# A hybrid decoder step: four sequences' states updated in one piece, and two read-outs turned together

## The chip, the cores and the metric

The kernel runs on one core of one Trainium2 chip. The core has five engines that run their own instruction queues beside each other: TensorE (PE, matmuls and transposes; PEld is its weight load), VectorE (DVE), ScalarE (ACT), GpSimd (POOL) and SyncE (SP), which here only issues transfers. Matmuls write into eight PSUM banks; everything else lives in SBUF or in HBM. The metric is the device time of one execution in microseconds (us), as the median of several runs.

## The reference

One layer of a decoder for a prompt of 1024 tokens and for 8 sample sequences of 8 tokens each, which bring their states along. A combined projection feeds a pooling branch and a Mamba-2 branch (SSD); both are gated and projected back. Cut to the part of the SSD that matters here:

```python
proj = h @ w_in                                   # 1024 -> 8224 columns
u_pool, z_pool, z_ssm, xbc, dt_raw, g_raw = split(proj)
xbc = silu(causal_conv(xbc)); xs, B, C = split(xbc)  # 32 heads of 64, 4 groups of B, C (128 states)
...
def step(h, inp):                                 # one chunk; for a sample: all its 8 tokens
    xq, dq, Bq, Cq = inp
    acs = cumsum(dq * Ag, axis=1)
    ...
    y = einsum('bijge,bjgep->bigep', att, xq)     # inside the chunk
    y = y + einsum('bign,bige,bgepn->bigep', Cq, exp(acs), h)          # read-out of the old state
    last = acs[:, -1]
    w_in = exp(last[:, None] - acs) * dq
    h = h * exp(last)[..., None, None] + einsum('bjgn,bjge,bjgep->bgepn', Bq, w_in, xq)   # update
    return h, y
```

For the 8 sample sequences the initial state `h` (8 × 32 heads × 64 × 128, 8 MB) is an input and the new one an output.

## The kernel before

The kernel goes through stages. First the input is normalised and split into high and low parts. Then the projection runs as Strassen products: `pair_w` loads two column blocks of the weights (`rawA`, three buffers, on SyncE's queue, L336), makes differences of them (L347, VectorE and GpSimd) and splits each into a rounded part `whi` (ScalarE, L145) and a rest `wlo` (GpSimd, L148); `product` (L410) makes two half products of twelve matmuls each, of 128×128 by 272 columns, into a PSUM bank, and VectorE adds the banks into the results (L419, L424). Banks come from three pools: `PA` (tag mm, three banks), `PB` (tag ps, four) and `PC` (tag pc, one). In this stage the half products take `PB` and `PA` in turn. Behind the projection come the prompt's SSD chunks, the branches' output projections (L221), the gates and the last projection (L2040 to L2042).

Beside the last ten pairs of columns of the projection, the generator `all_samples` is run: after each of some of the projection's steps it issues one more slot, up to its next `yield`, 28 slots in all. It computes the SSD of the 8 samples, group by group (four groups of B and C, each with 8 heads, so 512 columns of state for each sample), in two halves of four samples (`hf`):

- `load_h0(i)` loads the states of two samples (`h0`, 128 states × 2 × 512, two transfers on SyncE's queue, L1274); `begin` loads the group's rows; `rows` (L1285) turns x; `weigh` (L1294 to L1297) makes the weights inside the 8 tokens, `within` the part of the output from the tokens themselves.
- `spread(hf)` puts each sample's 8 columns of x and B into a stretch of 32 (GpSimd, L1307), and C's 8 columns into a zeroed `cz` of 4 × 32 (VectorE, L1309 and L1310). `split(hf)` turns x and B (L1318, L1320), scales them and rounds them with the rest beside them (L1322 to L1329) into a buffer of tag `dec`.
- `state(hf)` (L1344) multiplies the old states by `cz`: four samples, each 32 rows of one bank `PC`, of which 8 are of use. `out` (ScalarE, L1365) copies the bank, `end(hf)` turns it (four transposes, L1370), scales it (L1372) and adds it to the result (L1376), which goes out after the second half.
- `update(hf, e)` takes one half `e` of the heads, 256 columns: four 32-row matmuls (L1353) into four banks, GpSimd's multiplication of the old states by their decay (L1358), VectorE's adds from the banks (L1360), and the stores on ScalarE's queue (L1361).

TensorE's instructions stay in the order in which they are issued in this stage; on the other engines a scheduler places them within their dependencies. The slots before: `state(0)`, `out`, `update(0, 0)`; then `update(0, 1)`; then `end(0)`; then `state(1)`, `out`, `update(1, 0)`; then the next group's `rows` with `update(1, 1)` between; then `end(1)` at the head of the next group. `sp` is the pool in SBUF of the samples' buffers: three for `h0` (`H0B`), two for `dec`. Right behind the stage `ckt` takes the buffers of the chunks.

Of the kernel before, what the change touches and what calls it, by code (L numbers as in the profile page):

```python
# [9 lines left out]
F32R = mybir.dt.float32r  # L10
AF = mybir.ActivationFunctionType
ALU = mybir.AluOpType
# [8 lines left out]
P = 128  # L21
# [25 lines left out]
def tile_pool_ssd_step(  # L47
# [1049 lines left out]
        store_(new_conv[mc], t27)  # L1097
        yield 1

    H0B = 3  # L1100


    def dt_end():
# [161 lines left out]
    class Samples:  # L1265
# [23 lines left out]

        def weigh(self):  # L1290
            g, S, xb = self.g, NS, self.xb
            self.dec = dec = spt([P, 640], "dec", 2)[:S, :512].rearrange("p (h t) -> p h t", t=S)
            pc = PB()
            mm(pc[:S, :S], xb[:, 4], xb[:, 5], start=True, stop=True)  # L1294
            cb = pc[:S, S:2 * S]
            V.tensor_tensor(cb, pc[:S, :S], maskS.rearrange("p b i -> p (b i)"), ALU.mult)
            V.tensor_tensor(dec.rearrange("p h (b i) -> p h b i", i=8),  # L1297
                            Es[1][:, 8 * g:8 * g + 8].unsqueeze(2).to_broadcast([S, 8, NB, 8]),
                            cb.rearrange("p (b i) -> p b i", i=8).unsqueeze(1).to_broadcast([S, 8, NB, 8]), ALU.mult)

        def spread(self, hf):

            xb = self.xb
            rep = spt([P, 5, 4, 4, 8], "xw", 1)
            for b in range(4):
                o = 32 * hf + 8 * b
                nc.gpsimd.tensor_copy(rep[:, :, b], xb[:, 0:5, o:o + 8].unsqueeze(2).to_broadcast([P, 5, 4, 8]))  # L1307
            cz = spt([P, 4, 32], "cz", 2)
            V.memset(cz, 0.0)  # L1309
            V.tensor_copy(cz[:, :, 0:8], xb[:, 5, 32 * hf:32 * hf + 32].rearrange("p (b i) -> p b i", i=8))  # L1310
            self.half[hf] = rep, cz

        def split(self, hf):
            g = self.g
            rep, cz = self.half[hf]
            px = PB()
            for q in range(4):
                nc.tensor.transpose(px[:, q * P:(q + 1) * P], rep[:, q].rearrange("p b r i -> p (b r i)"), ident)  # L1318
# [3 lines left out]
            V.tensor_tensor(xs, px.rearrange("p (h d) -> p h d", d=64),  # L1322
                            wd3[:, hf, 8 * g:8 * g + 8].unsqueeze(2).to_broadcast([P, 8, 64]), ALU.mult)
            both = spt([P, 640], "dec", 2, F32R)
# [14 lines left out]
            V.tensor_tensor(t, inner(self.xd, self.dec, NS), t, ALU.add)  # L1339

        def state(self, hf):
            self.po = PC()
            for b in range(4):
                mm(self.po[32 * b:32 * b + 32, :], self.half[hf][2][:, b, :], self.h0[2 * hf + b // 2][:, b % 2], start=True, stop=True)  # L1344

        def update(self, hf, e):
            g = self.g
            xh, Bx, _ = self.half[hf]
            c = slice(256 * e, 256 * e + 256)
            pus = [p()[:, :256] for p in (PB, PA, PB, PA)]  # L1350
            for b in range(4):
                r = slice(32 * b, 32 * b + 32)
                mm(pus[b], Bx[r], xh[r, c], start=True, stop=True)  # L1353
            for i in range(2):
                j = 4 * hf + 2 * i
                h0 = self.h0[2 * hf + i]
                hv = h0[:, :, c].rearrange("p a (h d) -> p a h d", d=64)
                nc.gpsimd.tensor_tensor(hv, hv, ElS[:, j:j + 2, 8 * g + 4 * e:8 * g + 4 * e + 4].unsqueeze(3).to_broadcast([P, 2, 4, 64]), ALU.mult)  # L1358
                for a in range(2):
                    V.tensor_tensor(h0[:, a, c], h0[:, a, c], pus[2 * i + a], ALU.add)  # L1360
                store_(new_ssm_s[g, j:j + 2, :, c].rearrange("a p x -> p a x"), h0[:, :, c])  # L1361

        def out(self):
            self.yo = spt([P, 512], "hT", 1)
            act(self.yo, self.po, AF.Copy)  # L1365

        def end(self, hf):
            pn = PB()
            for q in range(4):
                nc.tensor.transpose(pn[:, q * P:(q + 1) * P], self.yo[:, q * P:(q + 1) * P], ident)  # L1370
            tn = spt([P, 4, 32], "tn", 1)
            V.tensor_tensor(tn.rearrange("p q (b i) -> p q b i", i=8),  # L1372
                            pn.rearrange("p (q b i) -> p q b i", q=4, i=32)[:, :, :, 0:8],
                            self.E2[:, :, 32 * hf:32 * hf + 32].rearrange("p q (b i) -> p q b i", i=8), ALU.mult)
            th = self.t[:, :, 32 * hf:32 * hf + 32]
            V.tensor_tensor(th, th, tn, ALU.add)  # L1376
            if hf:
                store_(ys_d[self.g], self.t)

    def all_samples():  # L1380
        gs_ = [Samples(g) for g in range(NG)]
        samples_load()
        gs_[0].begin()
        for i in range(2):
            gs_[0].load_h0(i)
        yield
        samples_decay()
        gs_[0].rows()
        gs_[0].spread(0)
        yield  # L1390
        gs_[0].split(0)
        gs_[0].weigh()
        yield
        for g, m in enumerate(gs_):
            n = gs_[g + 1] if g + 1 < NG else None
            if g:
                gs_[g - 1].end(1)
                m.split(0)
            m.within()
            if g:  # L1400
                m.load_h0(1)
# [24 lines left out]
            m.update(1, 1)  # L1426
            if n:
                n.weigh()
            yield
        gs_[-1].end(1)  # L1430
        yield

    def cc(m):
# [855 lines left out]
```

## Time and profile before

| | us |
|---|---|
| median of 3 runs | 1220.73 (1219.95 to 1222.36) |
| span of the profiled execution | 1219.3 |
| TensorE's busy time in it | 1203.2 |
| VectorE, GpSimd, ScalarE | 937.9, 758.1, 654.7 |

The profile is of one execution. Its rows have a start in us and a duration, then engine and line (L410 is line 410 of the kernel), the operation, result<-operands by the program's names, the shape, and a count of equal rows that were drawn together; brackets name idle time of the engine ahead of the row and what ended it. A row of a group has the count, the busy time, the mean of one in ns, and the idle time ahead. SPq is SyncE's queue of instructions, where transfers are issued. PEclk is the granted clock of TensorE, 1.00 for full.

### The profile page before, as it was taken

To read this page: it belongs to the slowest core of one execution; us is meant where nothing else is said; L and a number is where in the kernel's file an instruction comes from. 1 tells how busy PE (TensorE), PEld (TensorE's weight loads), DVE (VectorE), ACT (ScalarE), POOL (GpSimd) and SP (SyncE) were. 2 spreads that over 40 slices of the span, in tenths; PEclk is the share of its full clock that TensorE was granted. 3 is DMA by queue.
4 is the path that set the end of the run, shared out by engine and by line. 5 is a ranking of instruction groups with operands and counts; after the bars stand their busy time and mean duration, and the time that the engine had idled before them with its cause. 6 is when DMAs were issued, how large, how long until landed. Compare 5 with 4: busy or idle time off the path is not lost.

```text
span 1219.3 us, 25493 instructions
## 1 busy us (share of the span) xinstructions
PE 1203.2 (99%) x9330; PEld 1127.1 (92%) x9330; DVE 937.9 (77%) x1587; ACT 654.7 (54%) x1491; POOL 758.1 (62%) x677
## 2 busy tenths in 40 slices
PE   9999999999999999999999999999999999999997
PEld 8879999999999999999989899989888898999885
DVE  6993788877989578876676664686877889679976
ACT  6854366565656656454544344566676656312435
POOL 1137868875978778664676766155677758422661
PEclk9999999999999999999999999999999999999999
DMA  9835455564565545443656566898779888585794
GB/s 347 307 136 212 134 155 179 157 232 151 165 188 181 171 149 187 137 143 122 205 187 210 172 198 215 317 314 265 264 257 293 270 279 279 186 313 174 233 213 150
DMA packets 169845, 257.48 MB, mean 211 GB/s; under 512 B 32048, under 2 KB 88120, under 8 KB 169720
## 3 DMA queue, kind: packets, MB, share of 16 engines
q1 hardware_dynamic: 89256, 163.38, 40.3%
q10 hardware_dynamic: 78160, 88.27, 21.4%
q0 software_dynamic: 2304, 4.20, 2.0%
q8 instruction: 74, 1.21, 0.4%
q14 instruction: 51, 0.42, 0.1%
HBM read 170.69 MB, written 85.10 MB: 210 GB/s over the span
## 4 chain that ended last, share of the span: by engine, by line
PE 84%; DVE 6%; DMA 5%; ACT 3%; issue 1%; POOL 1%; SPq 0%; ACTq 0%; DVEq 0%
PE mm L410 23%; PE ps L410 23%; PE mm L221 14%; PE pc L410 5%; PE ps L1256 2%; PE pc L1542 2%; PE ps L2042 2%; PE ps L2040 2%; PE ps L2041 2%; PE ps L1259 2%; DMA wo<-ph 1%; DMA Y<-in_x_prompt 1%; DMA v<-ys 1%; DMA dec<-acs_d 1%; PE ps L1517 1%
## 5 line engine op out<-in xcount | busy, mean ns | idle before, releaser
L148 POOL TENSOR_TENSOR wlo<-rawA,whi 128x512 fp32r<-128x512 f32 x120 | 173.7, 1452 | 81.4 <-ACT whi L145 77.4
L221 PE MATMUL mm<-Y,whi 128*128 128x352 f32 (+1 forms) x960 | 195.7, 334 | 0.8 <-DVE G L1975 0.6
L148 POOL TENSOR_TENSOR wlo<-raw,whi 128x512 fp32r<-128x512 f32 x90 | 149.1, 1665 | 61.4 <-ACT whi L145 51.3
L221 PEld LDWEIGHTS mm<-Y,whi 128*128 128x128 f32 x960 | 159.1, 188 | 7.6 <-issue 4.6
L1088 DVE SCALAR_TENSOR_TENSOR GA<-GA,cvT,GA 128x1112 f32<-128x1112 f32 x72 | 133.8, 1863 | 0.1
L410 PE MATMUL mm<-Y,whi 128*128 128x272 f32 x800 | 119.0, 291 | 0.1
L410 PE MATMUL ps<-Y,whi 128*128 128x272 f32 x800 | 117.4, 289 | 0.0
L145 ACT ACTIVATE whi<-rawA 128x512 fp32r<-128x512 f32 x120 | 75.1, 627 | 76.1 <-PE ps L410 37.7
L145 ACT ACTIVATE whi<-raw 128x512 fp32r<-128x512 f32 x90 | 56.0, 629 | 98.9 <-DVE raw L347 35.2
L410 PEld LDWEIGHTS mm<-Y,whi 128*128 128x128 f32 x800 | 106.8, 188 | 1.8 <-DVE h L1360 0.3
L410 PEld LDWEIGHTS ps<-Y,whi 128*128 128x128 f32 x800 | 106.9, 188 | 0.8 <-issue 0.7
L221 PE MATMUL mm<-Y,wlo 128*128 128x352 f32 (+1 forms) x480 | 98.5, 327 | 0.0
L1244 ACT ACTIVATE dec<-dec,acT 128x128 f32<-128x128 f32 x256 | 78.8, 389 | 29.2 <-POOL dec L1240 29.2
L221 PEld LDWEIGHTS mm<-Y,wlo 128*128 128x128 f32 x480 | 81.7, 188 | 0.0
L1474 POOL TENSOR_TENSOR Y<-xb,Y 128x512 fp32r<-128x512 f32 x32 | 41.2, 1287 | 54.4 <-ACT Y L1472 54.4
L285 POOL TENSOR_TENSOR pw<-pw,ph 128x512 fp32r<-128x512 f32 x40 | 65.8, 1644 | 14.1 <-ACT ph L283 8.2
L410 PE MATMUL mm<-G,whi 128*128 128x272 f32 x480 | 71.4, 290 | 0.0
L410 PE MATMUL ps<-G,whi 128*128 128x272 f32 x480 | 70.4, 289 | 0.0
L410 PE MATMUL ps<-Y,wlo 128*128 128x272 f32 x400 | 66.6, 288 | 0.0
L410 PE MATMUL mm<-Y,wlo 128*128 128x272 f32 x400 | 66.6, 288 | 0.0
L410 PEld LDWEIGHTS mm<-G,whi 128*128 128x128 f32 x480 | 64.0, 188 | 0.9 <-issue 0.4
L410 PEld LDWEIGHTS ps<-G,whi 128*128 128x128 f32 x480 | 64.2, 188 | 0.4 <-issue 0.3
(582 smaller groups left out, 3172.9 us busy)
## 6 DMA issues: line engine op xcount, KB each, us to landing
rawA<-in_w_in SPq DMA_DIRECT2D x62, 512.0 KB
dec<-acs_d SPq DMA_DIRECT2D x32, 512.0 KB
xbc<-GA ACTq DMA_DIRECT2D x24, 512.0 KB
Y<-wo SPq DMA_DIRECT2D x10, 1024.0 KB
pw<-in_w_ssm_out ACTq DMA_DIRECT2D x32, 256.0 KB
ws<-ph ACTq DMA_DIRECT2D x32, 256.0 KB
ws<-pw ACTq DMA_DIRECT2D x32, 256.0 KB
h<-in_state_ssm SPq DMA_DIRECT2D x32, 256.0 KB
```

The lines of the kernel that those rows point to most:

```text
L145: ins = act(hi[:, :, :ncols], raw[:, :, :ncols], AF.Copy)
L148: (eng or nc.gpsimd).tensor_tensor(lo[:, :, :ncols], raw[:, :, :ncols], hi[:, :, :ncols].bitcast(F32), ALU.subtract)
L221: mm(ps[:, :n], w[k // 4][h][:, k % 4, :], r[k][:, o:o + n], start=(j == 0), stop=(j == len(terms) - 1))
L285: nc.gpsimd.tensor_tensor(raw.bitcast(F32R), raw, hi.bitcast(F32), ALU.subtract)
L410: mm(p, w[j // 8][:, k], A(k, s)[j // 4 == 1], start=(j == 0), stop=(j == 11))
L1088: V.scalar_tensor_tensor(d[:, :n], rp[:, k:k + n], cvT[:, 24 * k + mc:24 * k + mc + 1], d[:, :n], ALU.mult, ALU.add)
L1244: act(dec[:, h], dec[:, h], AF.Exp, bias=acT[:, c, 8 * g + h:8 * g + h + 1], scale=-1.0)
L1256: mm(o[hh], xd[:S, 2 * q + hh, :], dec[:S, 2 * q + hh], start=True, stop=state is None)
L1259: mm(o[hh], state[:, h * 64:h * 64 + 64], cE[:, h], start=False, stop=True)
L1474: nc.gpsimd.tensor_tensor(yl[g][:, :, o:o + S], v, yhc.bitcast(F32), ALU.subtract)
L1542: mm(pu, bt, xw.rearrange("p h d -> p (h d)"), start=True, stop=True)
L2040: mm(ps, hi, y[:, k, c0:c0 + cw], start=(first and k == 0), stop=False)
```

## The change

- `update(hf)` takes all 512 columns at once: four matmuls into four whole banks, four adds, two stores.
- It is issued later: `update(0)` stands behind `state(1)` of the same group, and `update(1)` behind `state(0)` of the next group; the last group's has a slot at the end.
- The decay is a function of its own, `decay(hf)`, issued behind `state(hf)`, ahead of that half's update.
- Both halves' read-outs go into one `PC` bank, `cz` having its 8 columns at place 0 for one half and at place 8 for the other, zeros elsewhere; the first half starts the sum and the second ends it. `out` and `end` come once for a group.
- `h0` has five buffers, `dec` three; `tn` holds 64 columns; the loads of the states move by a slot; `split(0)` of the first group comes a slot later.
- The tag `ph` is the first that `ckt` takes, and the space for descriptors of GpSimd's transfers is set to 1024.

```diff
-    H0B = 3
+    H0B = 5
...
-            self.dec = dec = spt([P, 640], "dec", 2)[:S, :512].rearrange("p (h t) -> p h t", t=S)
+            self.dec = dec = spt([P, 640], "dec", 3)[:S, :512].rearrange("p (h t) -> p h t", t=S)
...
-            V.tensor_copy(cz[:, :, 0:8], xb[:, 5, 32 * hf:32 * hf + 32].rearrange("p (b i) -> p b i", i=8))
+            V.tensor_copy(cz[:, :, 8 * hf:8 * hf + 8], xb[:, 5, 32 * hf:32 * hf + 32].rearrange("p (b i) -> p b i", i=8))
...
         def state(self, hf):
-            self.po = PC()
+            if hf == 0:
+                self.po = PC()
             for b in range(4):
-                mm(self.po[32 * b:32 * b + 32, :], self.half[hf][2][:, b, :], self.h0[2 * hf + b // 2][:, b % 2], start=True, stop=True)
-
-        def update(self, hf, e):
+                mm(self.po[32 * b:32 * b + 32, :], self.half[hf][2][:, b, :], self.h0[2 * hf + b // 2][:, b % 2],
+                   start=hf == 0, stop=hf == 1)
+
+        def decay(self, hf):
+            g = self.g
+            for i in range(2):
+                j = 4 * hf + 2 * i
+                hv = self.h0[2 * hf + i].rearrange("p a (h d) -> p a h d", d=64)
+                nc.gpsimd.tensor_tensor(hv, hv, ElS[:, j:j + 2, 8 * g:8 * g + 8].unsqueeze(3).to_broadcast([P, 2, 8, 64]), ALU.mult)
+
+        def update(self, hf):
...
-            pus = [p()[:, :256] for p in (PB, PA, PB, PA)]
+            pus = [p() for p in (PB, PA, PB, PA)]
...
-                mm(pus[b], Bx[r], xh[r, c], start=True, stop=True)
+                mm(pus[b], Bx[r], xh[r], start=True, stop=True)
...
                 for a in range(2):
-                    V.tensor_tensor(h0[:, a, c], h0[:, a, c], pus[2 * i + a], ALU.add)
-                store_(new_ssm_s[g, j:j + 2, :, c].rearrange("a p x -> p a x"), h0[:, :, c])
+                    V.tensor_tensor(h0[:, a], h0[:, a], pus[2 * i + a], ALU.add)
+                store_(new_ssm_s[g, j:j + 2].rearrange("a p x -> p a x"), h0)
...
-        def end(self, hf):
+        def end(self):
...
-            tn = spt([P, 4, 32], "tn", 1)
...
+            tn = spt([P, 4, NS], "tn", 1)
+            for hf in range(2):
+                c = slice(32 * hf, 32 * hf + 32)
+                V.tensor_tensor(tn[:, :, c].rearrange("p q (b i) -> p q b i", i=8),
+                                pn.rearrange("p (q b i) -> p q b i", q=4, i=32)[:, :, :, 8 * hf:8 * hf + 8],
+                                self.E2[:, :, c].rearrange("p q (b i) -> p q b i", i=8), ALU.mult)
+            V.tensor_tensor(self.t, self.t, tn, ALU.add)
+            store_(ys_d[self.g], self.t)
...
             m.state(0)
-            m.out()
-            m.update(0, 0)
-            yield
-            m.update(0, 1)
             m.spread(1)
-            m.load_h0(2)
+            if o:
+                o.update(1)
+            m.decay(0)
             yield
             m.load_h0(3)
-            m.end(0)
+            yield
             m.split(1)
...
             m.state(1)
             m.out()
-            m.update(1, 0)
+            m.update(0)
+            m.decay(1)
...
-            m.update(1, 1)
-            if n:
                 n.weigh()
+                n.load_h0(1)
+            else:
+                m.update(1)
...
-    for shape, tag, bufs in (((P, P), "bt", 2), ((P, 8, 64), "xd", 2), ((P, 8, 64), "xw", 1), ((P, 512), "ph", 3),
+    for shape, tag, bufs in (((P, 512), "ph", 3), ((P, P), "bt", 2), ((P, 8, 64), "xd", 2), ((P, 8, 64), "xw", 1),
...
-    nc = _bacc.Bacc("TRN2", target_bir_lowering=False, num_devices=1)
+    nc = _bacc.Bacc("TRN2", target_bir_lowering=False, num_devices=1, dynamic_dma_scratch_size=1024)
```

TensorE before, from group 0's first read-out on (`pc` is the read-out's bank, `ps` and `mm` the banks of update groups and half products, `dec` the update's operands):

```order
L1344 MATMUL pc_8296<-h_1268_7981,cz_8032 32x512 x2
L1344 MATMUL pc_8296<-h_1269_7984,cz_8032 32x512 x2
L1353 MATMUL ps_8303<-dec_8108 128x256
L1353 MATMUL mm_8304<-dec_8108 128x256
L1353 MATMUL ps_8305<-dec_8108 128x256
L1353 MATMUL mm_8306<-dec_8108 128x256
L410 MATMUL mm_8319<-Y_1096,whi_8150 128x272 x8
L410 MATMUL mm_8319<-Y_1096,wlo_8151 128x272 x4
L410 MATMUL ps_8333<-Y_1096,whi_8150 128x272 x8
L410 MATMUL ps_8333<-Y_1096,wlo_8151 128x272 x4
L1353 MATMUL ps_8347<-dec_8108 128x256
L1353 MATMUL mm_8348<-dec_8108 128x256
```

The first half's heads are updated behind the read-out, the second half's behind the next two half products. TensorE of the change, from the second half's read-out of the same group on:

```order
L1345 MATMUL pc_8299<-h_1307_8225,cz_8309 32x512 x2
L1345 MATMUL pc_8299<-h_1325_8342,cz_8309 32x512 x2
L1361 MATMUL ps_8520<-dec_8202 128x512
L1361 MATMUL mm_8521<-dec_8202 128x512
L1361 MATMUL ps_8522<-dec_8202 128x512
L1361 MATMUL mm_8523<-dec_8202 128x512
L410 MATMUL mm_8539<-Y_517,whi_8189 128x272 x4
L410 MATMUL mm_8539<-Y_518,whi_8189 128x272 x4
```

Now the first half's update, at full width, stands behind the second half's read-out; behind the first read-out stands none. VectorE before, at group 0's first update (`u` and `s` are the projection's sums, `h` the states):

```order
L1309 MEMSET cz_8663 128x128
L1310 COPY cz_8663<-hst_8463 128x4x8
L1360 TENSOR_TENSOR h_1268_7981<-h_1268_7981,ps_8303 128x256
L1360 TENSOR_TENSOR h_1268_7981<-h_1268_7981,mm_8304 128x256
L419 TENSOR_TENSOR u_1314_8265<-s_1313_8264,mm_8319 128x272
L1360 TENSOR_TENSOR h_1269_7984<-h_1269_7984,ps_8305 128x256
L1360 TENSOR_TENSOR h_1269_7984<-h_1269_7984,mm_8306 128x256
```

VectorE of the change, at the update of the same samples:

```order
L424 TENSOR_TENSOR u_1316_8269<-u_1316_8269,mm_8465 128x272
L424 TENSOR_TENSOR u_1316_8269<-u_1316_8269,ps_8480 128x272
L347 TENSOR_TENSOR rawA_8261<-rawA_8261,rawA_8259 128x512
L1309 MEMSET cz_8780 128x128
L1366 TENSOR_TENSOR h_1268_7981<-h_1268_7981,ps_8520 128x512
L1310 COPY cz_8780<-hst_8423 128x4x8
L1366 TENSOR_TENSOR h_1268_7981<-h_1268_7981,mm_8521 128x512
L1366 TENSOR_TENSOR h_1269_7984<-h_1269_7984,ps_8522 128x512
L1366 TENSOR_TENSOR h_1269_7984<-h_1269_7984,mm_8523 128x512
L424 TENSOR_TENSOR u_1315_8268<-u_1315_8268,mm_8539 128x272
```

The four whole-bank adds stand together, with a weight difference, the zeroing and the copy of the next `cz` ahead of them and among them. SyncE's queue of the change, for about one group (`rawA` are weights, `hst` a group's rows):

```order
L1274 DMA h_1325_8342<-in_state_ssm 128x512 x2
L1274 DMA h_1358_8536<-in_state_ssm 128x512 x2
L336 DMA rawA_8259<-in_w_in 128x1024
L1279 DMA hst_8976<-xbs_174 128x384
L336 DMA rawA_8261<-in_w_in 128x1024
L336 DMA rawA_8570<-in_w_in 128x1024
L1274 DMA h_1377_8630<-in_state_ssm 128x512 x2
L1274 DMA h_1389_8703<-in_state_ssm 128x512 x2
L336 DMA rawA_8572<-in_w_in 128x1024
```

Two loads of states stand ahead of the last weight load shown. Before, two also stood ahead of a weight load in each group; what moved is that their buffers are now two of five, not of three, and that the update and its stores which give a buffer free are issued later than before.

More of the change, by code (lines that the diff above doesn't have):

```diff
@@ L1323, in split @@
                             wd3[:, hf, 8 * g:8 * g + 8].unsqueeze(2).to_broadcast([P, 8, 64]), ALU.mult)
-            both = spt([P, 640], "dec", 2, F32R)
+            both = spt([P, 640], "dec", 3, F32R)
             xh, Bx = both[:, :512], both[:, 512:]
@@ L1370, in end @@
                 nc.tensor.transpose(pn[:, q * P:(q + 1) * P], self.yo[:, q * P:(q + 1) * P], ident)
-            tn = spt([P, 4, 32], "tn", 1)
[L1372 to L1378, printed above, removed]
+            tn = spt([P, 4, NS], "tn", 1)
[6 more added lines that the diff above has]
+            store_(ys_d[self.g], self.t)
     def all_samples():
@@ L1390, in all_samples @@
         yield
-        gs_[0].split(0)
         gs_[0].weigh()
@@ L1394, in all_samples @@
         for g, m in enumerate(gs_):
+            o = gs_[g - 1] if g else None
             n = gs_[g + 1] if g + 1 < NG else None
-            if g:
-                gs_[g - 1].end(1)
-                m.split(0)
+            if o:
+                o.end()
+            m.split(0)
             m.within()
-            if g:
-                m.load_h0(1)
+            m.load_h0(2)
             yield
             m.state(0)
-            m.out()
-            m.update(0, 0)
-            yield
-            m.update(0, 1)
             m.spread(1)
-            m.load_h0(2)
+            if o:
+                o.update(1)
+            m.decay(0)
             yield
             m.load_h0(3)
-            m.end(0)
+            yield
             m.split(1)
@@ L1425, in all_samples @@
                 n.spread(0)
-            m.update(1, 1)
-            if n:
                 n.weigh()
+                n.load_h0(1)
+            else:
+                m.update(1)
             yield
-        gs_[-1].end(1)
+        gs_[-1].end()
         yield
```

3 lines of the change are left out of this document (removed).

## The prediction

> **What bounds the kernel now.** I read the page from the top: span, busy time by engine, the chain that ended last. Then the windows by stage, for what bounds the stage that the change touches; then TensorE's timeline around the work that changes.
>
> ```profile
> span 1219.3 us, 25493 instructions
> PE 1203.2 (99%) x9330; PEld 1127.1 (92%) x9330; DVE 937.9 (77%) x1587; ACT 654.7 (54%) x1491; POOL 758.1 (62%) x677
> ...
> PE 84%; DVE 6%; DMA 5%; ACT 3%; issue 1%; POOL 1%; SPq 0%; ACTq 0%; DVEq 0%
> ```
> ```profile
> core 0: us, PE busy (x) PEld busy (x) DVE busy (x) ACT busy (x) POOL busy (x), PEclk, DMA share, GB/s
> 565.00:765.00 200.00, 199.66 (x1638) 186.35 (x1637) 123.05 (x274) 90.42 (x189) 127.91 (x124) 1.00 0.59 196
> 900.00:1000.00 100.00, 98.35 (x780) 86.63 (x780) 82.46 (x140) 64.56 (x170) 70.16 (x81) 1.00 0.87 288
> ```
>
> TensorE is busy 99% of the span and makes 84% of the chain. The samples' state work lies in 565 to 765 us, where TensorE is busy 199.66 of 200 us at the full granted clock and VectorE, ScalarE and GpSimd are busy 123, 90 and 128. So in this stage the program advances by TensorE time alone: an instruction taken out of TensorE's queue there is worth what it takes in that queue, and work saved elsewhere is worth nothing. Since "busy" can hide slow issue, I take the cost of a group not from its duration but from how much later the projection's next matmul starts.
>
> ```profile
> 591.20 0.67 PE L410 MATMUL mm<-Y,wlo 128*128 128x272 f32 x4
> ...
> 592.72 0.67 PE L410 MATMUL ps<-Y,wlo 128*128 128x272 f32 x4
> 593.32 1.07 PE L1344 MATMUL pc<-h,cz 128*32 128x512 f32 x8
> 594.31 0.38 PE L1353 MATMUL ps<-dec 32*128 32x256 f32 x1
> ...
> 594.63 1.27 PE L410 MATMUL mm<-Y,whi 128*128 128x272 f32 x8
> 595.74 0.67 PE L410 MATMUL mm<-Y,wlo 128*128 128x272 f32 x4
> ...
> 597.24 0.66 PE L410 MATMUL ps<-Y,wlo 128*128 128x272 f32 x4
> 597.83 0.38 PE L1353 MATMUL ps<-dec 32*128 32x256 f32 x1
> ...
> 598.15 1.26 PE L410 MATMUL mm<-Y,whi 128*128 128x272 f32 x8
> 599.26 0.66 PE L410 MATMUL mm<-Y,wlo 128*128 128x272 f32 x4
> ```
>
> Twelve projection matmuls take 592.72 − 591.20 = 1.52 us undisturbed, 0.127 each. A state read-out with the update group behind it stands between 592.72 and 595.74: 3.02 − 1.52 = 1.50 us for both. An update group that stands alone: 599.26 − 597.24 = 2.02, less 1.52, is **0.50**. The update behind a read-out adds only 594.63 − 594.31 = **0.32**, since the change of tile shape is already paid.
>
> **The change, part by part.** *Update groups.* Before, 16 groups of four 32-row matmuls, 256 columns wide; now 8 groups 512 wide. Seven of the eight that stay stand behind a read-out and one, the last, alone, as one did before. So eight go: four that stood alone, the one behind group 0's first read-out, and three that stood among the next group's transposes:
>
> ```profile
> 619.33 0.38 PE L1353 MATMUL ps<-dec 32*128 32x256 f32 x1
> ...
> 619.85 0.33 PE L1294 MATMUL ps<-hst 128*64 128x64 f32 x2
> ...
> 698.26 0.38 PE L1353 MATMUL ps<-dec 32*128 32x256 f32 x1
> ...
> 698.60 0.33 PE L1294 MATMUL ps<-hst 128*64 128x64 f32 x2
> ```
>
> There a group takes 0.52 and 0.34; I take the mean, 0.43. Removed: 4 × 0.50 + 3 × 0.43 + 0.32 = 3.61 us. All at the dearest row is 8 × 0.52 = 4.16, all at the cheapest 8 × 0.32 = 2.56.
>
> *Their width.* The eight that stay carry 256 more columns. This form is not in the trace; the nearest row is the pitch of 512-column matmuls against that of 272:
>
> ```profile
> 1132.02 0.40 PE L2040 MATMUL ps<-Y,a11h 128*128 128x512 f32 x1
> 1132.25 0.40 PE L2041 MATMUL ps<-Y,a11h 128*128 128x512 f32 x1
> ```
>
> 0.23 − 0.127 = 0.10 for 240 columns, so 0.11 for 256, if the four row tiles stream side by side as their equal starts show. From above: the eight 512-column tile matmuls of the read-out take 594.31 − 593.32 = 0.99, two sets of four, so 0.25 for 256 columns. From below 0, if the group is bound by its issue. I take 0.11, because the update's operands are of the projection's type: 8 × 0.11 = 0.88 (0 to 2.0) added.
>
> *Read-outs and turns.* The read-out has as many matmuls as before; only their bank is shared, so it costs nothing more. Of eight sets of four transposes four go:
>
> ```profile
> 604.26 0.60 PE L1370 MATMUL ps<-ident,hT 128*128 128x128 f32 x4
> 604.70 0.60 PE L1318 MATMUL ps<-ident,xw 128*128 128x128 f32 x4
> ```
>
> One set is 604.70 − 604.26 = 0.44; four are 1.76 us. [...]
>
> **The sum** on TensorE is −3.61 + 0.88 − 1.76 = **−4.5 us**, bounds −2.56 + 2.0 − 1.76 = −2.3 and −4.16 + 0 − 1.76 = −5.9.
>
> *Off TensorE*, costed at nothing behind a TensorE that never stands still:
>
> ```profile
> L1360 DVE TENSOR_TENSOR h<-h,ps 128x256 f32<-128x256 f32 x32 | 13.2, 412 | 4.1 <-POOL h L1358 4.1
> L1322 DVE TENSOR_TENSOR xw<-ps,wd 128x512 f32<-128x512 f32 x8 | 5.4, 677 | 0.0
> L347 DVE TENSOR_TENSOR raw<-rawA 128x512 f32<-128x512 f32 x7 | 9.1, 1294 | 0.9 <-DMA rawA<-in_w_in 0.9
> L1310 DVE COPY cz<-hst 128x32 f32<-128x32 f32 x6 | 4.1, 679 | 0.2
> ...
> L1358 POOL TENSOR_TENSOR h<-h,ElS 128x512 f32<-128x512 f32 x32 | 33.3, 1073 | 0.0
> ```
>
> A half's adds become four of about 0.68 (the 512-wide one of L1322) for eight of 0.41: 2.7 for 3.3 us. GpSimd's decay keeps its 32 × 1.07 us of elements in 16 longer instructions, now one to three slots ahead of the adds that need it, so VectorE's 4.1 us of waiting on it goes. ScalarE makes four copies for eight, and 32 stores of 256 KB become 16 of 512 KB. All run on engines with 70 us or more free of these 200. If that cover goes, the bank wait below is the price. The smaller descriptor space bears on transfers that GpSimd issues, 16 of them at the end, the last one here:
>
> ```profile
> 1180.35 1.83 POOL L2065 DMA_DIRECT2D top<-in_x_prompt  x1
> ...
> 1212.90 1.02 POOL L2186 TENSOR_TENSOR m<-m,s1h 128x256 f32<-128x256 f32 x1 [19.30 <-ACT G L2184]
> ```
>
> GpSimd idles 19.3 us before its last work, which covers a delay of the 1.83 us kind; 0 taken, 0 to +1.8 bounds, inside the range that follows. After the stage the order of instructions is the same, so what TensorE gains should shift all that follows.
>
> The span is then 1219.3 − 4.5 = 1214.8. The median of the runs, 1220.73, lies 1.43 above the span, so I forecast 1214.8 + 1.4 = **1216.2 us**; with the bounds, 1214.8 to 1218.4.
>
> **The rivals.** *A bank wait in place of the removed work (slower).* A half's update now fills four whole banks in one slot, two of three of the "mm" kind. The next projection products take 1.52 us each and alternate kinds, so the third, 3.04 us after the update, needs the bank of the update's first "mm" matmul, which VectorE's second add frees. VectorE's order now has a weight difference (L347, up to 1.40), the zeroing and a copy for the next half among these adds:
>
> ```profile
> 612.70 0.17 DVE L1309 MEMSET cz<- 128x128 f32 x1
> 612.90 1.01 DVE L1310 COPY cz<-hst 128x32 f32<-128x32 f32 x1
> ```
>
> At worst 1.40 + 0.17 + 1.01 + 2 × 0.68 = 3.94 us, 0.90 late; at every one of eight updates 7.2 us, so 1216.2 + 7.2 = **1223.4**. Break-even is 4.5 / 8 = 0.56 late per update; slower than before by over 0.2% (2.4 us, about what this measurement can tell from no change) from 0.87. At the means (1.29, 0.68) it is 0.46 late, 1219.9. Against: VectorE can start on that queue while the 1 us read-out ahead of the update still runs, which takes off more than the 0.90; and its 4.1 us wait in the update before cost TensorE next to nothing. [...] Chance 0.09.
>
> *Weights late behind the states' loads.* On SyncE's queue a weight load of each group stands behind two state loads, and such loads wait for the stores of an update, which now comes later.
>
> ```profile
> SPq L1274 <- DMA out<-h: 51.3, 12, 7.9
> ```
> ```profile
> 576.54 0.37 SPq L336 DMA_DIRECT2D rawA<-in_w_in  x1
> ...
> 646.81 0.33 SPq L336 DMA_DIRECT2D rawA<-in_w_in  x1
> ```
> ```profile
> 582.02 0.69 DVE L347 TENSOR_TENSOR raw<-rawA 128x512 f32<-128x512 f32 x1 [0.88 <-DMA rawA<-in_w_in]
> ...
> 657.52 1.38 DVE L347 TENSOR_TENSOR raw<-rawA 128x512 f32<-128x512 f32 x1
> ```
>
> A weight load lands 582.02 − 576.54 = 5.5 us after issue and elsewhere is used after 10.7, so 5.2 us of cushion. Such waits last 51.3 / 12 = 4.3 us on average, 7.9 at most: nothing late at the mean, 2.7 at most. Half of that at three changes of group is 4.1 us given back: **1220.3**, the same as before. For it: the stores are twice as large and come in one piece. Against: five buffers for three, and TensorE did not wait for weights before, with waits of that length. Chance 0.08.
>
> *The gain is lost at the stage's end.* If the first chunks' loads come when they came before, because something other than TensorE releases them, all 4.5 us go: **1220.7**.
>
> ```profile
> 741.43 0.33 SPq L1236 DMA_DIRECT2D dec<-acs_d  x1
> ```
> ```profile
> 769.50 1.09 PE L221 MATMUL mm<-Y,whi 128*128 128x384 f32 x5 [0.25 <-DVE Y L1573]
> ```
>
> For it: the first chunk's load is issued at 741.43, while the last projection products still run, and the DMA share later is 0.87. Against: at the chunks' start TensorE waits only 0.25 us, and for VectorE, not for a load. Chance 0.05.
>
> **How the numbers follow.** Forecast, inside its bounds, 0.75; a larger gain than the bounds (a tile change that costs more than the rows show) 0.03; same, from the two rivals that give the gain back, 0.13; slower, the bank wait, 0.09. Faster by over 0.2% is thus 0.78. The range goes from the larger bound, 1214.8, to the late weights' 1220.3, which leaves out less than 2 in 10.
>
> **What would show it.** In the changed profile: eight update groups and four sets of transposes gone, a read-out with its 512-wide update at 1.5 + 0.11 = 1.6 us in TensorE's timeline, 0.44 us for a turn, and the sample stage's end some 4.5 us earlier, with no new idle time before L410. The bank wait would show as TensorE (or its weight loads) idle on VectorE's L1366; late weights as L347 idle on a transfer into rawA and then L410 on ScalarE or GpSimd; the lost gain as a chunk loop that starts earlier but idles longer. I am wrong in size if a 512-wide group costs far more than 0.11 above the narrow one.

## The result, and the profile after

The changed kernel takes **1214.58 us** (median of 5 runs, 1213.64 to 1215.85) where the kernel before took 1221.67 beside it (5 runs, 1219.95 to 1222.82): a ratio of 0.9944, 95% interval 0.9932 to 0.9957, or 6.8 us less (5.3 to 8.3). The forecast was 4.5 us less. The page of the changed kernel, the same rows as before:

```profile
span 1212.6 us, 25285 instructions
PE 1198.2 (99%) x9282; PEld 1122.4 (93%) x9282; DVE 929.1 (77%) x1551; ACT 652.1 (54%) x1487; POOL 756.9 (62%) x661
...
PE 81%; DVE 7%; DMA 4%; ACT 4%; issue 2%; POOL 1%; ACTq 0%; SPq 0%; DVEq 0%; POOLq 0%
```

TensorE still bounds it, with 48 fewer matmuls and transposes. Where the time went I read by cutting TensorE's timeline at the starts of matmuls that both kernels have: the first of the samples' preparation (L1181), the last of the projection (L410), the last inside the chunks (L1256), the last of all, and then the end of the span. Worked out so from the traces, in us, for all kernels run:

| kernel | start | sample stage | chunks | output stages | end | span |
|---|---|---|---|---|---|---|
| before | 561.3 | 204.96 | 286.64 | 158.3 | 8.1 | 1219.3 |
| before, again (c1) | 561.8 | 205.57 | 286.77 | 158.3 | 8.1 | 1220.5 |
| changed | 560.7 | 200.30 | 285.35 | 158.3 | 7.9 | 1212.6 |
| changed, again (c2) | 561.1 | 200.31 | 284.43 | 158.3 | 8.2 | 1212.3 |
| e1 side parts alone | 560.8 | 204.94 | 286.58 | 158.3 | 9.1 | 1219.7 |
| e2 `ph` not first | 561.4 | 200.30 | 290.59 | 158.3 | 9.9 | 1220.4 |
| e3 update alone | 561.2 | 202.52 | 286.23 | 158.3 | 9.0 | 1217.3 |
| e4 read-out alone | 561.3 | 203.40 | 285.48 | 158.3 | 7.9 | 1216.3 |
| e5 narrow pairs | 560.2 | 200.53 | 284.96 | 158.3 | 7.7 | 1211.7 |
| e6 decay beside | 560.3 | 200.29 | 284.74 | 158.3 | 7.9 | 1211.6 |
| e8 two passes | 560.5 | 215.35 | 285.23 | 158.3 | 8.2 | 1227.5 |
| e9 other tags first | 560.9 | 200.29 | 284.26 | 158.3 | 7.9 | 1211.7 |
| e10 stores as before | 560.7 | 200.26 | 284.18 | 158.3 | 9.6 | 1213.0 |

The sample stage is **4.7 us** shorter, close to the forecast sum. The chunks are 1.3 us shorter, which I had not expected; the 0.6 us at the start lies inside what the start varies by from one execution to the next (560.2 to 561.8, for kernels that are the same up to there). TensorE's timeline of the changed kernel at group 0's second read-out, and in the slot of the next group's transposes:

```profile
608.91 0.67 PE L410 MATMUL ps<-G,wlo 128*128 128x272 f32 x4
609.51 1.06 PE L1345 MATMUL pc<-h,cz 128*32 128x512 f32 x8
610.50 0.49 PE L1361 MATMUL ps<-dec 32*128 32x512 f32 x1
...
610.94 1.28 PE L410 MATMUL mm<-Y,whi 128*128 128x272 f32 x8
...
617.09 0.60 PE L1285 MATMUL ps<-ident,hst 128*64 128x128 f32 x4
617.62 0.33 PE L1294 MATMUL ps<-hst 128*64 128x64 f32 x2
```

The read-out starts at 609.51 and the projection goes on at 610.94: 1.43 us, where before it was 594.63 − 593.32 = 1.31 with an update of half the width. So a group twice as wide costs 0.12 more. In the second stretch the update that stood between the transposes (L1285) and L1294 is gone.

### The profile page after: what moved, and what is told of

Read it like the earlier page. It is cut to its first block, busy times and chain, and to the rows that moved or that the text cites. A ratio compares the mean times of both kernels' runs of the same rounds, so it can differ in the third digit from the quotient of the medians.

```text
span 1212.6 us, 25285 instructions
## 1 busy us (share of the span) xinstructions
PE 1198.2 (99%) x9282; PEld 1122.4 (93%) x9282; DVE 929.1 (77%) x1551; ACT 652.1 (54%) x1487; POOL 756.9 (62%) x661
## 4 chain that ended last, share of the span: by engine, by line
PE 81%; DVE 7%; DMA 4%; ACT 4%; issue 2%; POOL 1%; ACTq 0%; SPq 0%; DVEq 0%; POOLq 0%
PE mm L410 23%; PE ps L410 23%; PE mm L221 14%; PE pc L410 5%; PE ps L1256 2%; PE pc L1547 1%; PE ps L1259 1%; PE ps L2047 1%; PE ps L2046 1%; PE ps L2045 1%; DMA Y<-in_x_prompt 1%; DMA dec<-acs_d 1%; PE ps L956 1%; PE ps L1522 1%; DVE tf L642 1%
## 5 line engine op out<-in xcount | busy, mean ns | idle before, releaser
L410 PE MATMUL mm<-Y,whi 128*128 128x272 f32 x800 | 118.7, 290 | 0.0
L410 PE MATMUL ps<-Y,whi 128*128 128x272 f32 x800 | 117.5, 289 | 0.0
L410 PEld LDWEIGHTS mm<-Y,whi 128*128 128x128 f32 x800 | 106.9, 188 | 2.5 <-issue 1.0
L410 PEld LDWEIGHTS ps<-Y,whi 128*128 128x128 f32 x800 | 107.1, 188 | 0.8 <-issue 0.7
L410 PE MATMUL mm<-G,whi 128*128 128x272 f32 x480 | 71.5, 291 | 0.0
L410 PE MATMUL ps<-G,whi 128*128 128x272 f32 x480 | 70.3, 289 | 0.0
L410 PE MATMUL mm<-Y,wlo 128*128 128x272 f32 x400 | 66.6, 288 | 0.0
L410 PE MATMUL ps<-Y,wlo 128*128 128x272 f32 x400 | 66.5, 288 | 0.0
L410 PEld LDWEIGHTS mm<-G,whi 128*128 128x128 f32 x480 | 64.0, 188 | 1.3 <-issue 1.1
L410 PEld LDWEIGHTS ps<-G,whi 128*128 128x128 f32 x480 | 64.2, 188 | 0.3 <-issue 0.3
```

The source lines that it names most:

```text
L410: mm(p, w[j // 8][:, k], A(k, s)[j // 4 == 1], start=(j == 0), stop=(j == 11))
```

## The experiments

Each kernel is an edit of the kernel before or of the changed one, and every ratio is to runs of the kernel before on the same chip: e1 to e4 on one chip, e5 to e9 on another, c1 and c2 on a third, e10 by itself.

**e1: the side parts alone** (`ph` first and the descriptor space, in the kernel before).

```diff
-    for shape, tag, bufs in (((P, P), "bt", 2), ((P, 8, 64), "xd", 2), ((P, 8, 64), "xw", 1), ((P, 512), "ph", 3),
+    for shape, tag, bufs in (((P, 512), "ph", 3), ((P, P), "bt", 2), ((P, 8, 64), "xd", 2), ((P, 8, 64), "xw", 1),
...
+    nc = _bacc.Bacc("TRN2", target_bir_lowering=False, num_devices=1, dynamic_dma_scratch_size=1024)
```

> The kernel before with only the two side parts of the change: ph taken first behind the sample stage, and the descriptor space of 1024. The order of instructions on every engine is that of before. Theory (stage): the change is worth what leaves TensorE's queue in the sample stage (4.7 us in the traces of before and after), and the 2 us beyond it are scatter of the start and of waits in the chunks: here then no difference, within 1.5 us, and TensorE's sample stage as long as before. Rival (side parts): they take away waits at the chunks, 1.3 us in those two traces: here 1.3 to 2.4 us faster, with TensorE's waits before L1519 and L1256 gone.

Measured: ratio 1.0006 (0.9997 to 1.0014). By themselves the side parts are worth nothing, and the chunks take 286.58 us as before.

**e2: the changed kernel with `ph` in its old place.**

```diff
-    for shape, tag, bufs in (((P, 512), "ph", 3), ((P, P), "bt", 2), ((P, 8, 64), "xd", 2), ((P, 8, 64), "xw", 1),
+    for shape, tag, bufs in (((P, P), "bt", 2), ((P, 8, 64), "xd", 2), ((P, 8, 64), "xw", 1), ((P, 512), "ph", 3),
```

> The changed kernel with ph taken in its old place. Theory (stage): as the changed kernel, 4.7 to 7 us faster than before. Rival (side parts): the chunks' waits come back, 1.3 us or more lost, so 3.5 to 5.5 us faster than before.

Measured: 1221.07 us, ratio 1.0005 (0.9996 to 1.0014). **The whole gain is gone**, more than either theory had. The sample stage is as short as in the changed kernel, 200.30; the chunks begin with a stall. VectorE's timeline there (start, duration, instruction, idle time before it), then TensorE's and ScalarE's, then windows (TensorE's granted clock is the third figure from the end of a row, the share of the DMA engines' time the second):

```profile
762.33 2.49 DVE L1578 TENSOR_TENSOR Y<-Y,Y 128x1088 fp32r<-128x1088 f32 x2
771.11 0.69 DVE L1533 TENSOR_TENSOR xd<-ps,dtT 128x512 f32<-128x512 f32 x1 [6.28 <-DMA gs<-u]
771.71 0.68 DVE L1535 TENSOR_TENSOR xw<-ps,wdT 128x512 f32<-128x512 f32 x1
772.31 1.41 DVE L1730 TENSOR_TENSOR R<-mm,R 128x384 f32<-128x384 f32 x3
```
```profile
766.44 1.44 PE L221 MATMUL mm<-Y,whi 128*128 128x352 f32 x8
767.72 0.80 PE L221 MATMUL mm<-Y,wlo 128*128 128x352 f32 x4
768.36 0.80 PE L221 MATMUL mm<-Y,whi 128*128 128x352 f32 x4
772.91 0.99 PE L221 MATMUL mm<-Y,whi 128*128 128x384 f32 x4 [3.76 <-DVE R L1730]
...
774.99 1.48 PE L221 MATMUL mm<-Y,whi 128*128 128x384 f32 x4
776.27 1.02 PE L1522 MATMUL ps<-ident,xb 128*128 128x128 f32 x4
```
```profile
765.60 0.34 ACTq L501 DMA_DIRECT2D gs<-u  x1
768.95 0.28 ACT L1527 ACTIVATE bt<-ps 128x128 f32<-128x128 f32 x1 [3.62 <-DMA gs<-u]
```
```profile
766.00:768.00 2.00, 2.00 (x14) 2.00 (x13) 0.00 (x0) 0.00 (x0) 0.00 (x0) 1.00 0.98 358
768.00:772.00 4.00, 1.16 (x8) 0.87 (x6) 0.89 (x2) 3.02 (x7) 0.00 (x0) 1.00 1.06 395
772.00:774.00 2.00, 1.09 (x5) 1.09 (x6) 2.00 (x5) 2.00 (x6) 0.00 (x0) 0.93 0.59 237
774.00:776.00 2.00, 2.00 (x8) 2.00 (x8) 0.85 (x1) 1.75 (x4) 1.99 (x2) 0.50 0.00 0
776.00:780.00 4.00, 4.00 (x25) 3.90 (x24) 1.67 (x3) 4.00 (x15) 0.15 (x1) 0.86 0.35 139
```

The chain is this: the projection's last gate values `u` are stored to `gs`, the last of them from 765.60 on, with the DMA engines full (0.98 and more). VectorE's first instruction of the chunks, into `xd`, waits for such a store 6.28 us, and ScalarE's first, into `bt`, waits 3.62 us; nothing in the program's data ties `xd` or `bt` to `gs`, so I take the tie to be the place in memory, that of a `u` which is still being stored. The traces hold no addresses. Behind the instruction into `xd` on VectorE's queue stands L1730, which empties the output projection's banks, and TensorE waits 3.76 us for that. Then it runs at half clock (0.50 in the window from 774 to 776): four matmuls of 384 columns from 774.99 to 776.27 take 1.28 us, as long as eight of 352 columns took at 766.44. In the kernel before, in the changed kernel and in e9 (in this order) the same instruction starts without a wait:

```profile
769.36 0.68 DVE L1528 TENSOR_TENSOR xd<-ps,dtT 128x512 f32<-128x512 f32 x1
```
```profile
764.10 0.68 DVE L1533 TENSOR_TENSOR xd<-ps,dtT 128x512 f32<-128x512 f32 x1
```
```profile
764.31 0.68 DVE L1533 TENSOR_TENSOR xd<-ps,dtT 128x512 f32<-128x512 f32 x1
```

The kernel before takes the tags in the same order as e2 and has no such wait. So the order alone does not make it; what e2 has besides is the samples' new code, with five `h0` and three `dec` buffers where there were three and two, and the smaller descriptor space.

**e9: other tags first**, as a test of that reading: not `ph`, but `xd` in another place.

```diff
-    for shape, tag, bufs in (((P, 512), "ph", 3), ((P, P), "bt", 2), ((P, 8, 64), "xd", 2), ((P, 8, 64), "xw", 1),
-                             ((P, 4, NS), "szs", 1), ((P, 512), "t2", 1), ((P, 512), "hst", 2)):
+    for shape, tag, bufs in (((P, 4, NS), "szs", 1), ((P, 512), "t2", 1), ((P, 512), "hst", 2),
+                             ((P, P), "bt", 2), ((P, 8, 64), "xd", 2), ((P, 8, 64), "xw", 1), ((P, 512), "ph", 3)):
```

> The changed kernel with szs, t2 and hst taken first behind the sample stage, then bt, xd, xw and ph last: not the order of the change, but also one in which xd does not come to lie where the last products' results are still being stored from. Theory (place in memory): VectorE's L1533 no longer waits for the store gs<-u (6.28 us in the trace with bt and xd first), TensorE's wait behind it is gone, and the time is the changed kernel's, 5 to 7 us below before. Rival (ph itself must come first): as with ph in its old place, no faster than before.

Measured: 1214.85 us, ratio 0.9950 (0.9938 to 0.9963): the changed kernel's time, with `ph` last. So `ph` need not come first: it counts where the tags come to lie, and the wait before `xd` is gone. As e9 moves all the tags, that `xd` alone decides is not shown.

**e3: the update's part alone** (from the changed kernel), and **e4: the read-out's part alone** (from the kernel before). In e3 `cz`, `start`, `stop` and `end(hf)` also are as before the change, in e4 as in the changed kernel.

```diff
e3
         def state(self, hf):
-            if hf == 0:
-                self.po = PC()
+            self.po = PC()
...
             m.state(0)
+            m.out()
...
+            m.end(0)
             m.split(1)
e4
         def state(self, hf):
-            self.po = PC()
+            if hf == 0:
+                self.po = PC()
...
             m.state(0)
-            m.out()
...
-            m.end(0)
```

> The changed kernel with a bank, a copy and a turn for each half's read-out again: the update's part of the change alone. Theory (stage): four sets of transposes come back, 4 x 0.44 = 1.76 us; the sample stage is 2.9 us shorter than before, and the time 2.9 us below before plus the same scatter as the changed kernel's, so 1.8 us above the changed kernel. Rival (the shared bank is what matters, through copies and VectorE): about all of the gain goes, within 1 us of before.

> The kernel before with the shared read-out bank and one turn for a group, the updates as before. Theory (stage): 4 x 0.44 = 1.76 us less in TensorE's sample stage, 1.8 us faster. Rival (the shared bank matters more than its transposes): 4 us or more faster. If the later read-out makes other work late: no gain.

Measured: e3 0.9977 (0.9968 to 0.9986), 2.8 us less; e4 0.9982 (0.9973 to 0.9991), 2.2 us less. In the sample stage the update's part is worth 204.96 − 202.52 = 2.4 us and the read-out's 204.96 − 203.40 = 1.6, which add to 4.0 of the 4.7. Of the missing 0.7, about 0.5 is one place of e3, where TensorE's L1256 waits 0.42 us for VectorE's L419, as it does not in the changed kernel; e4 has a like wait of 0.2 us before L1294.

**e5: the update as pairs of narrow groups**, in the new slots.

```diff
-            for b in range(4):
-                r = slice(32 * b, 32 * b + 32)
-                mm(pus[b], Bx[r], xh[r], start=True, stop=True)
+            for e in range(2):
+                c = slice(256 * e, 256 * e + 256)
+                for b in range(4):
+                    r = slice(32 * b, 32 * b + 32)
+                    mm(pus[b][:, c], Bx[r], xh[r, c], start=True, stop=True)
```

> The changed kernel with each 512-column matmul of an update as two of 256 into the same bank, in the same slot: 16 groups again, at the new places. Theory (what a group costs is its start and end, not its columns): the second group of a slot costs about what one behind a read-out did, 0.3, where the 256 more columns cost 0.12, so 8 x 0.2 = 1.5 us longer than the changed kernel's sample stage, 5.2 us below before. Rival (columns count, groups are cheap when they stand together): no difference from the changed kernel, all of the gain lies in the place.

Measured: 0.9956 (0.9943 to 0.9969), and a sample stage of 200.53, 0.23 us above the changed kernel's and not 1.5. TensorE's timeline:

```profile
609.01 1.06 PE L1345 MATMUL pc<-h,cz 128*32 128x512 f32 x8
610.01 0.38 PE L1363 MATMUL ps<-dec 32*128 32x256 f32 x1
...
610.23 0.28 PE L1363 MATMUL ps<-dec 32*128 32x256 f32 x1
...
610.45 1.26 PE L410 MATMUL mm<-Y,whi 128*128 128x272 f32 x8
```

From the read-out to the projection it is 610.45 − 609.01 = 1.44 us, as with one wide group. A second group right behind one of its own shape adds 610.45 − 610.01 − 0.32 = 0.12 us, a group behind a read-out 0.32, a group alone in the projection 0.50. My expectation was wrong: the update's part of the gain comes **from the place, not from the number** of its matmuls or their width. The three places differ in how many changes of tile shape (128×128, 128×32, 32×128 in the rows) the group adds to TensorE's stream: none, one and two. If that is what tells them apart, a change costs about 0.2 us here, an estimate from these three figures; no run shows a change by itself. The update's part of the change takes away 15 of them, two with each of the four lone groups and the three among the transposes, and one behind group 0's first read-out: 3.0 us, where the terms measured 2.9 (3.9 less 8 × 0.12, below). One group among the transposes cost only 0.34 and does not fit.

**e6: the decay issued with the update.**

```diff
         def update(self, hf):
             xh, Bx, _ = self.half[hf]
+            self.decay(hf)
```

> The changed kernel with the states' decay issued with the update, as before, not a slot or more ahead. Theory (bank wait): VectorE's adds now start behind a GpSimd instruction of 2.1 us, so the second bank comes free 2 us later; in the changed kernel's trace the third half product finds its bank free 1.0 to 1.6 us ahead (0.06 at the last update). So TensorE waits 0.5 to 1 us at seven updates and 2 at the last: 5.5 to 9 us lost, no faster than before. Rival (as before the change, where VectorE's 4.1 us of waiting cost TensorE nothing): within 1 us of the changed kernel.

Measured: 0.9933 (0.9920 to 0.9946), the changed kernel's time and stage. But this does not test the price of a late decay, since GpSimd's instructions come as early as in the changed kernel. The groups of L1353 (durations, then first and last start) of the changed kernel and of e6:

```profile
L1353 POOL TENSOR_TENSOR h<-h,ElS x16: 1899/1904/2351, 594.7 to 725.8; 128x1024 f32<-128x1024 f32 x16
```
```profile
L1353 POOL TENSOR_TENSOR h<-h,ElS x16: 1896/1904/2350, 594.8 to 725.4; 128x1024 f32<-128x1024 f32 x16
```

Counted from the start of the sample stage, all sixteen start within 0.5 us of each other in the two kernels. So writing it as a step of its own was not needed here; that the update itself comes later is enough.

**e8: the update's adds in two passes**, the rival of the prediction made by force.

```diff
-                    V.tensor_tensor(h0[:, a], h0[:, a], pus[2 * i + a], ALU.add)
+                    V.tensor_tensor(pus[2 * i + a], h0[:, a], pus[2 * i + a], ALU.add)
+                    V.tensor_copy(h0[:, a], pus[2 * i + a])
```

> The changed kernel with the adds of the update in two passes, into the bank and then out of it into the states: VectorE's work on each bank doubled, 4 x 0.67 us more for a half. The order has the four adds first, so the second bank comes free after the sixth pass, some 2.4 us later than now. Theory (bank wait, with 1.0 to 1.6 us of slack at seven updates and 0.06 at the last): TensorE waits 0.8 to 1.4 us at each of the seven and 2.3 at the last, 8 to 12 us above the changed kernel, slower than before. Rival (VectorE has a third of the stage free and catches up): within 2 us of the changed kernel.

Measured: 1229.14 us, ratio 1.0060 (1.0046 to 1.0075), slower than before; the sample stage is 15.1 us longer than the changed kernel's. TensorE's timeline behind one update:

```profile
631.41 0.50 PE L1361 MATMUL ps<-dec 32*128 32x512 f32 x1
...
631.84 1.28 PE L410 MATMUL mm<-G,whi 128*128 128x272 f32 x8
...
633.46 1.17 PE L410 MATMUL ps<-G,whi 128*128 128x272 f32 x8
634.47 0.67 PE L410 MATMUL ps<-G,wlo 128*128 128x272 f32 x4
636.93 0.36 PE L410 MATMUL mm<-G,whi 128*128 128x272 f32 x1 [1.79 <-DVE h L1367]
```

Two half products run, and the third, into a bank of the kind "mm", waits for VectorE's L1367: the place is the one that the rival named, and it is 1.8 us late. The size, 15 us for 8 to 12 expected, comes from a second price. The windows behind that wait, and those of 10 us around it and around a shorter one (granted clock third from the end):

```profile
634.00:636.00 2.00, 1.14 (x10) 0.92 (x8) 2.00 (x4) 0.00 (x0) 2.00 (x2) 1.00 0.01 4
636.00:638.00 2.00, 1.07 (x8) 1.10 (x9) 2.00 (x5) 0.43 (x1) 0.22 (x1) 0.96 0.17 55
638.00:640.00 2.00, 2.00 (x11) 2.00 (x10) 1.68 (x4) 1.04 (x2) 0.00 (x0) 0.50 0.89 330
```
```profile
630.00:640.00 10.00, 8.21 (x57) 6.79 (x57) 9.16 (x17) 2.53 (x5) 5.45 (x3) 0.89 0.44 158
640.00:650.00 10.00, 10.00 (x78) 10.00 (x78) 3.89 (x7) 5.01 (x12) 6.85 (x5) 0.94 0.61 218
650.00:660.00 10.00, 8.84 (x70) 7.39 (x69) 8.49 (x17) 2.37 (x5) 7.33 (x8) 1.00 0.36 125
...
740.00:750.00 10.00, 8.03 (x53) 7.44 (x52) 9.01 (x17) 2.99 (x6) 1.37 (x2) 0.85 0.41 154
750.00:760.00 10.00, 10.00 (x80) 10.00 (x80) 4.34 (x8) 3.87 (x9) 6.94 (x6) 0.98 0.68 228
```

TensorE is idle for 10.0 us in all at nine places of the stage, within what the theory had, and behind the two longest waits, of 1.79 and 1.97 us, its granted clock falls (to 0.50 from 638 to 640), which by the windows of 10 us loses 10 × (0.11 + 0.06 + 0.15 + 0.02) = 3.4 us more. The idle time is counted from the end of the last matmul's row, some 0.29 us after its start; in an undisturbed stream the next one starts 0.127 after it. Counted from there, the nine waits are 11.5 us, and with the 3.4 they make 14.9 of the 15.1.

**c1 and c2: both kernels again.** They are the two files unchanged.

> The kernel before, unchanged: a second look. In the profiles of the two kernels the time falls into start (561.3 and 560.7 us), sample stage (205.0 and 200.3), chunks (286.6 and 285.4), output stages (158.3 both) and the end behind the last matmul (8.1 and 7.9). Theory (scatter): the chunks' 1.3 us are scatter of two executions, so the chunks come out anywhere from 284.3 to 286.7 here. Rival (the chunks gain too): 286.6 again, within 0.3.

> The changed kernel, unchanged: a second look. Theory (scatter): the sample stage is 200.3 us again, the chunks and the start as scattered as in the kernel before, and the time 4.7 us below it give or take 1.5. Rival (the chunks gain too): chunks at 285.4 or below, 1.3 us or more under those of the kernel before in the same call, and 6 us or more between the medians.

Measured: c1 0.9996 (0.9987 to 1.0005); c2 0.9946 (0.9933 to 0.9958), 6.6 us less. The chunks took 286.77 and 284.43 us. The rival holds: the chunks' part of the gain comes again. TensorE's waits in the chunks, of the kernel before and of c1 (line waited for, releaser, us in total, times, longest):

```profile
PE ps L1519 <- DVE cE L1537: 1.6, 1, 1.6
PE ps L1256 <- DVE cE L1537: 0.7, 1, 0.7
```
```profile
PE ps L1519 <- DMA xb<-xbc: 1.6, 1, 1.6
...
PE ps L1256 <- DVE cE L1537: 0.9, 1, 0.9
```

and of the changed kernel (c2 has neither):

```profile
PE ps L1256 <- ACT bt L1527: 0.4, 1, 0.4
...
PE ps L1256 <- DVE cE L1542: 0.2, 1, 0.2
```

Two stalls of 2.3 and 2.5 us together are shorter or gone. So it is in all the runs but e2, which has a stall of its own: TensorE's idle time in the chunks is 2.6 to 2.8 us in the kernel before, c1 and e1, 2.0 in e3, 1.5 in e4, and 0.3 to 1.2 in the changed kernel, c2, e5, e6, e8, e9 and e10. What is left of the chunks when it is taken off is 283.8 to 284.3 us in all of these. The chunks' part of the gain is thus idle time of TensorE, not less work.

**e10: the states stored in halves**, as before the change.

```diff
-                store_(new_ssm_s[g, j:j + 2].rearrange("a p x -> p a x"), h0)
+                for e in range(2):
+                    c = slice(256 * e, 256 * e + 256)
+                    store_(new_ssm_s[g, j:j + 2, :, c].rearrange("a p x -> p a x"), h0[:, :, c])
```

> The changed kernel with the new states stored in halves of the heads, 32 transfers of 256 KB as before instead of 16 of 512 KB. So far the chunks took 286.6 to 286.8 us in three profiles with the updates of before and both read-outs turned apart, and 284.3 to 285.4 in five of the changed kernel and its near variants, whatever the sample stage took. Theory (stores: their number or their pieces bear on how later transfers are served): chunks at 286.2 or more, 1.5 us or so of the gain lost. Rival (nothing to do with the stores): chunks at 284.3 to 285.4 and the changed kernel's time; then the cause of the chunks' part stays open.

Measured: 0.9946 (0.9930 to 0.9963), chunks 284.18 us. The number and size of the stores have nothing to do with it.

## Why the prediction was right, and where not

*The sum on TensorE.* Forecast −4.5 us, measured −4.7 in the sample stage, so the cost from how much later the projection goes on, and not from durations, was the right way to count. Term by term, by the same reading at all places: the groups that went were worth 3.9 us for 3.61 forecast (one that stood alone cost 0.66, and two of the three among the transposes 0.52); the width 0.12 a group for 0.11; the turns 4 × 0.44 = 1.76 as forecast.

*The reason for it* was half right. The prediction counted groups that vanish and columns that are added. e5 has as many groups as before and nearly all of the gain all the same: by the estimate from e5 (0.12, 0.32 and 0.50 us for a group) what is paid is mainly each change of tile shape in TensorE's stream, about 0.2 us, and the change takes those away. The prediction's 0.32 behind a read-out was then not a group whose change of shape was already paid, but one that adds one change in place of two.

*Off TensorE.* That VectorE, GpSimd and the stores cost nothing in the stage held: no new idle time before L410, with TensorE busy 199.75 of the 200 us from 565 on. The bank wait did not come: in the changed kernel's trace the second bank is free 1.1 to 1.7 us before the third half product starts at seven updates, and 0.15 at the last (from the end of VectorE's second add to the start of TensorE's first matmul into the bank). e8 shows that the wait comes at the place that the rival said once VectorE is late enough, and that it costs its own length (1.79 us in the timeline above) and, behind the two longest, 1.7 us each by a lower clock besides. The late weights did not come either, although a wait of a state load for its stores reached 13.8 us, where the prediction took 7.9 as the most: no wait of TensorE shows in the stage. The early decay, for which the prediction gave VectorE 4.1 us less of waiting, needed no step of its own (e6).

*The step that failed* is the sentence that "what TensorE gains should shift all that follows". It fails twice. First, that the gain reached the end was luck as far as the prediction goes: with `ph` in its old position all of it is lost (e2), to a wait of VectorE for a store, which I put down to memory that `xd` takes over. The changed kernel escapes by the order of the tags, an edit that the prediction had not priced at all. I gave the rival at the stage's end 0.05 and looked at loads into the chunks; in e2 it was a store out of the stage before, and VectorE's queue that carried it to TensorE. Second, the chunks themselves became 1.3 to 2.3 us shorter, by idle time of TensorE that went, on which the forecast had nothing; this puts the measured median, 1214.58, just past the range's lower end of 1214.8.

*What stays open* is why TensorE waits less in the chunks. Three profiles with the kernel before or its side parts alone have 286.6 to 286.8 us there; all six with both parts and without e2's stall 284.2 to 285.4 (changed, c2, e5, e6, e9, e10), and e8, with its sample stage of 215 us, 285.2. So neither the length of the sample stage, nor the stores, nor the place of the tags by itself does it. e4 alone has 285.5, e3 286.2, with one profile each. Which of the two parts carries it, and through what, was not settled.

## What to carry to other kernels

A small matmul of another tile shape in a full TensorE stream cost here, by the estimate from e5, mainly the changes of shape that it made (0.50 us for a group alone, 0.12 behind one of its own shape): put it behind work of its own shape before making it wider or fewer. Where a stage is shortened, ask of the first instruction of the next stage what its buffer's memory was last used for: in e2 VectorE's first instruction of the chunks waited 6.28 us for a store, where the same instruction of the kernel before waited for none, and VectorE's queue carried the wait on to TensorE as 3.76 us; that memory was the tie is my reading and not shown. An engine that is off the path may still hold a bank (in e8 TensorE waited 1.79 us for VectorE's L1367): count from the end of the matmul to the next use of that bank, and what stands ahead in the emptying engine's queue.

## What the runs showed that was not expected

Behind a wait of 1.79 us in e8 TensorE's granted clock fell to 0.50 (from 638 to 640), and behind one of 1.97 us it fell as well (means of 0.85 and 0.98 in the windows from 740 to 760), while six of 0.63 to 1.19 us in the same stage left it at 1.00. In e2 it fell to 0.50 behind a wait of 3.76 us (from 774 to 776). The waits of 1.6 us in the chunks of the kernel before and of c1 left it at 1.00. Each of the three falls cost 1.7 us by the windows above, whatever the length of the wait ahead of it: 10 × (0.11 + 0.06) and 10 × (0.15 + 0.02) in e8, 2 × 0.07 + 2 × 0.50 + 4 × 0.14 in e2. Whether it is their length that tells these few waits apart, or something else, is not shown.

A second group of four 32-row matmuls right behind one of its own shape cost 0.12 us (e5), about as much as one undisturbed projection matmul of 272 columns, 0.127.
